# Own slots for the modulation weights in two feed-forward stages of a hybrid backbone kernel

## The chip, the cores and the metric

The kernel is one program on one core of a Trainium2 chip. The metric is device time in microseconds (us) of one execution. TensorE (PE) does the matrix products, VectorE (DVE), ScalarE (ACT) and GpSimd (POOL) the elementwise work, and SyncE (SP) issues all the transfers, in one queue. Each engine runs its instructions in a fixed order: an instruction that waits holds up all that stand behind it on the same engine.

## The reference

Two layers of a diffusion backbone over 256 context tokens and 256 latent tokens of width 1024. Each layer has a feed-forward sub-layer, a token mixer (four branches, one of which is the diagonal state space "S5") and a second feed-forward sub-layer. Every sub-layer is preceded by a modulated norm and followed by a gated norm:

```python
def modulated_norm(x, g, shift, scale):
    return rms_norm(x, g) * (1 + scale) + shift

def swiglu(h, w_in, w_out):
    a, b = jnp.split(h @ w_in, 2, axis=-1)
    return (jax.nn.silu(a) * b) @ w_out

def ffn_sublayer(x, mods, base, g_pre, g_post, w_in, w_out):
    h = modulated_norm(x, g_pre, mods[base], mods[base + 1])
    return x + 0.5 * mods[base + 2] * rms_norm(swiglu(h, w_in, w_out), g_post)
...
    for i in range(DEPTH):
        ...
        mod_l = (act_l @ w_mod[i] + b_mod[i])[:, None, :]
        mod_c = (act_c @ w_mod[i][:, :n_c] + b_mod[i][:n_c])[None, None, :]
```

The shifts, scales and gates (`mods`) are nine vectors of 1024 for the latents; the context has nine in layer 0 and five in layer 1. They come from products of one vector with the columns of `w_mod`. The hidden width of a feed-forward is 2816.

## The kernel before

The program runs the stages one after the other: layer 0's first feed-forward, layer 0's mixer, layer 0's second feed-forward (called **stage B** here, after the pool name in the code), layer 1's first feed-forward (**stage C**), layer 1's mixer, layer 1's second feed-forward. The change touches stages B and C.

A feed-forward stage has a first half over 22 blocks of 128 hidden columns, numbered f (function `ffn`). One block takes two weight chunks (`fin`, 512 KB each, 128x1024), and a product in split precision: each chunk is cut into a high part (`wh`, on ACT, L218) and a low part (`wl`, on DVE, L219), and TensorE makes three products per 128 rows (L225 to L227, tile `pin`): 48 matmuls of 128x512 per block. Then `gate` makes the gated value on ACT and DVE (tiles `t` and `gg`, L484 to L486, L230, L232). The second half (`outproj`, tile `y`) multiplies by the output weights (`foa`, `fob`), and `boundary` adds the residual row (`xr`, loaded from `xd`) and makes the norm for the next stage.

Three loads share this time:

- **The raw ring.** `wchunk` and, before the change, `mod_steps` too take their landing tiles from the same pool (`rp`, tag `raw`, 4 slots). A slot is free again when the work on the tile in it is done; the split tiles `wh` and `wl` have 3 slots each.
- **Modulation products** (`mod_steps`): one step loads a 512 KB piece of `w_mod` and multiplies it with the broadcast activation. In stage B (5 of the 9 vectors, 40 steps) both streams are wanted: the latents' product with its sum is one DVE instruction (tile `jk`, L271), the context's is a product on POOL (L276, in place) and then a sum on ACT (L277), after which the slot is free. In stage C (the other 4, 32 steps) only the latents are wanted: even pieces go to DVE, odd pieces to POOL and ACT. `stepper` hands the steps out by weight: 50 of the stage's 60 units, after two skipped calls.
- **S5 tables** (`s5_tables`, mostly POOL): eight slices, each with four pieces of work ("yields"). The first makes `bb` and `vv` (L1079 to L1090, POOL), the second `wt` (POOL), the third a small TensorE product of `bb` and `vv` (`pn`, L1102) with its copies and `rot`, the fourth turns `wt` on TensorE (L1129), copies it to `row` and stores `row` (1728 KB, `s5tabd`). `row` has one buffer, so the next slice's first write (L1085) waits for that store. `ahead` advances this by one yield per call of `step`, one call for each f.

TensorE's order is the program's own (`manual_schedule`); on the other engines and in SP's queue a scheduler orders the instructions.

Of the kernel before, what the change touches and what calls it, by code (L numbers as in the profile page):

```python
# [9 lines left out]
F32 = mybir.dt.float32  # L10
# [6 lines left out]
P = 128  # L17
D = 1024
KT = 8
# [144 lines left out]
def build(tc, A):  # L164
# [20 lines left out]
    with st, tc.manual_schedule(engines={mybir.EngineType.PE}):  # L185
# [68 lines left out]
            dma(ngt[l], A["ng"][l])  # L254
            dma(bmt[l], A["bmod"][l])

        def mod_steps(l, js, act, raw=None):
            if callable(act):
                act = act()
            for j in js:  # L260
                ss = [1] if l == 1 and j >= 5 else [0, 1]
                for k in range(KT):
                    w = raw() if raw else rp.tile([P, D], F32, tag="raw", name="raw")
                    dma(w, A["wmod"][l, j, k])
                    c = j * KT + k
                    both = l == 0 and j >= JB
                    for s in ss if both else [1]:
                        if 0 not in ss and k % 2:
                            continue
                        jk = sp.tile([P, D], BF16, tag="sq", name="jk", bufs=1)  # L270
                        V.scalar_tensor_tensor(  # L271
                            jk, w, 0.5, act[s], op0=ALU.mult, op1=ALU.mult, accum_out=md[l][:, s, c : c + 1]
                        )
                    if not both and (0 in ss or k % 2):
                        s = ss[0]
                        G.tensor_tensor(w, w, act[s], op=ALU.mult)  # L276
                        S.activation(w, w, AF.Copy, scale=0.5, accum_out=md[l][:, s, c : c + 1])  # L277
                    n = 4 if raw else KT
                    if (k + 1) % n == 0:
                        for s in ss:  # L280
                            m = md[l][:, s, c + 1 - n : c + 1]
                            V.tensor_tensor(m, m, bmt[l][:, c + 1 - n : c + 1], op=ALU.add)
                    yield
# [187 lines left out]

            return run

        def ffn(l, i, h, late, toks, nxt, gp, step, rows, fill, begun=()):
            g = []
            begun = list(begun)
            cs_all = slice(min(toks) * P, NTOK)
# [46 lines left out]
                return gp((n_[0] - 1) // 8).tile([P, 2, 512], F32R, tag="gg", name="wf", bufs=8).rearrange("p a b -> p (a b)")  # L524

            fill()
            return outproj(lhs, NF, A["foa"][l, i], A["fob"][l, i], toks, nxt, lambda: gp(3), place, step)


        xp = pool(st, "xp", 2)  # L530
# [12 lines left out]
        tabd = dp.tile([P, 8, S5_ROW], F32, name="s5tabd")  # L543
        sds = [dp.tile([4, 32, 240], F32, name=f"s5sd{i}") for i in range(8)]

        def ahead(stack, gp, name, slices):

            gp(0)
            gp(1)
            ts = ExitStack()  # L550
            tq = ts.enter_context(tc.tile_pool(name=name, bufs=1, reuse_waits="tile"))
            gen = s5_tables(E, L - 1, slices, tabd, sds, tq, lambda: psy.tile([P, 512], F32, tag="py", name="pn"))

            def close():
                for _ in gen:
                    pass
                ts.close()

            gp.before[2] = close
            return gen  # L560

        def stepper(gens, total, skip=0):

# [32 lines left out]
        with ExitStack() as fs:  # L596
            with ExitStack() as s0:
# [22 lines left out]
                for t in TALL:  # L620
                    xs0[t] = tp.tile([P, D], F32, name=f"x0_{t}")
                raw0 = lambda: tp.tile([P, D], F32, tag="raw0", name="raw0", bufs=RAW0)
                ms0 = mod_steps(0, [0], act, raw0)
                pm = [psy.tile([P, 512], F32, tag="py", name="pm1") for _ in range(2)]

                def rows0(t, load=True):
# [111 lines left out]
        for l in range(L):  # L738
# [8 lines left out]
            with ExitStack() as fs:  # L747
                gp = Gates(fs, f"B{l}")
                if last:
                    n3 = dict(src=xd, out=A["out"], keep=[])  # L750
                    ffn(l, 1, h, late, toks, n3, gp, lambda w: None, lambda: gate_rows(l, 6, 5, 0.5, streams), lambda: None)
                else:
                    n3 = dict(src=xd, out=None, keep=TALL)

                    def fill1():
                        n3.update(coeff=pre_coeff(1, 0, 0, [0, 1]), h=new_h())

                    st1 = stepper([(mod_steps(1, [0, 1, 2, 3, 4], act_load), 40)], 50, 2)
                    tg1 = ahead(fs, gp, "s5p", range(0, 4))

                    def step1(w):
                        st1(w)
                        next(tg1, None)

                    late = ffn(l, 1, h, late, toks, n3, gp, step1, lambda: gate_rows(l, 6, 5, 0.5, streams), fill1)
                    h = n3["h"]
            if not last:
                with ExitStack() as fs:
                    gp = Gates(fs, "C")
                    n4 = dict(src=xd, out=None, keep=TLAT)  # L770

                    def fill2():
                        n4.update(coeff=pre_coeff(1, 3, 2, [0, 1]), h=new_h())

                    st2 = stepper([(mod_steps(1, [5, 6, 7, 8], act_load), 32)], 50, 2)
                    tg2 = ahead(fs, gp, "s5q", range(4, 8))

                    def step2(w):
                        st2(w)
                        next(tg2, None)  # L780

                    late = ffn(1, 0, h, late, TALL, n4, gp, step2, lambda: gate_rows(1, 0, 1, 0.5, [0, 1]), fill2)
                    h = n4["h"]


# [1330 lines left out]
```

## Time and profile before

| | us |
|---|---|
| median of three runs (2684.0 to 2690.7) | 2684.12 |
| the profiled execution | 2686.32 |
| its span, first to last instruction | 2684.5 |
| TensorE busy | 2511.3 (94%) |
| VectorE busy | 1701.1 (63%) |
| ScalarE busy | 1095.2 (41%) |
| GpSimd busy | 792.0 (30%) |

The profiled execution is 2.2 us above the median of the runs. Busy shares are means over stages with different limits; a stage has to be read by itself. TensorE's ends are modelled, so its busy time includes matmuls that ran at the lower of its two clock levels.

### The profile page before, as it was taken

What the parts mean: (1) busy time and instruction counts of PE and PEld (TensorE: products, weight loads), DVE (VectorE), ACT (ScalarE), POOL (GpSimd) and SP (SyncE); (2) the same over time, 40 slices, a digit from 0 to 9 for tenths busy, and PEclk for the clock granted to TensorE, in tenths of its full rate; (3) what the DMA queues carried; (4) which work ended last, traced back from release to release, by engine and by line L of the source; (5) the groups of instructions that cost most, each with busy time, mean ns of one, the idle gap of its engine ahead of it and who ended that gap; (6) DMA issues with size and microseconds to landing.
All of it is one profiled execution on the core that took longest, in us unless ns stands there. A gap on an engine that the chain in (4) does not pass through costs nothing. (4 is left out here: it accounts for less than half of the span.)

```text
span 2684.5 us, 38045 instructions
## 1 busy us (share of the span) xinstructions
PE 2511.3 (94%) x14606; PEld 2105.2 (78%) x14606; DVE 1701.1 (63%) x2488; ACT 1095.2 (41%) x1876; POOL 792.0 (30%) x696
## 2 busy tenths in 40 slices
PE   6978899999999898999888999999999999888998
PEld 3856777888788776888667788887889889788997
DVE  6788885455646798557676646455435567666564
ACT  5435322454543233444343334333334565235443
POOL 4884100100101874007795315554101012000000
PEclk8989999999999999999999999999999999999999
DMA  6345666222232233343554553555532335766564
GB/s 235 107 148 185 210 227 212 83 79 74 78 109 79 77 98 103 94 165 128 183 191 160 175 196 128 182 200 170 196 133 75 95 118 181 263 212 217 158 191 146
DMA packets 137090, 406.87 MB, mean 152 GB/s; under 512 B 27223, under 2 KB 46408, under 8 KB 134092
## 3 DMA queue, kind: packets, MB, share of 16 engines
q1 hardware_dynamic: 136908, 404.44, 45.7%
q8 instruction: 115, 1.88, 0.3%
q14 instruction: 67, 0.55, 0.1%
HBM read 372.31 MB, written 32.06 MB: 151 GB/s over the span
## 5 line engine op out<-in xcount | busy, mean ns | idle before, releaser
L219 DVE TENSOR_TENSOR wl<-raw,wh 128x1024 fp32r<-128x1024 f32 x424 | 572.2, 1350 | 467.7 <-ACT wh L218 461.0
L218 ACT ACTIVATE wh<-raw 128x1024 fp32r<-128x1024 f32 x424 | 447.4, 1056 | 512.8 <-issue 127.4
L227 PE MATMUL pin<-hh,wl 128*128 128x512 f32 (+1 forms) x1468 | 535.0, 364 | 62.1 <-DVE wl L219 62.1
L225 PE MATMUL pin<-hh,wh 128*128 128x512 f32 (+1 forms) x1468 | 534.9, 364 | 12.6 <-DVE hh L353 7.7
L226 PE MATMUL pin<-hl,wh 128*128 128x512 f32 (+1 forms) x1468 | 531.1, 362 | 4.1 <-DVE hl L356 4.0
L227 PEld LDWEIGHTS pin<-hh,wl 128*128 128x128 f32 x1468 | 283.8, 193 | 117.9 <-DVE wl L219 78.2
L246 POOL TENSOR_TENSOR r<-v,mhalf 128x1 f32<-128x1 f32 (+2 forms) x46 | 32.0, 696 | 1046.5 <-DVE v L245 947.9
L225 PEld LDWEIGHTS pin<-hh,wh 128*128 128x128 f32 x1468 | 284.0, 193 | 58.2 <-DVE hh L353 9.2
L276 POOL TENSOR_TENSOR raw<-raw,act 128x1024 f32<-128x1024 f32 x88 | 242.9, 2762 | 266.3 <-DVE jk L271 149.8
L226 PEld LDWEIGHTS pin<-hl,wh 128*128 128x128 f32 x1468 | 284.0, 193 | 46.4 <-DVE hl L356 6.3
L271 DVE SCALAR_TENSOR_TENSOR jk<-raw,act 128x1024 bf16<-128x1024 f32 x152 | 209.0, 1375 | 154.7 <-DMA raw<-wmod 146.6
L1211 PE MATMUL pm<-hh,wh 128*128 128x512 f32 (+1 forms) x704 | 252.2, 358 | 0.0
L1213 PE MATMUL pm<-hh,wl 128*128 128x512 f32 (+1 forms) x704 | 245.5, 349 | 0.8 <-DVE wl L219 0.8
L1212 PE MATMUL pm<-hl,wh 128*128 128x512 f32 (+1 forms) x704 | 245.5, 349 | 0.0
L277 ACT ACTIVATE raw<-raw 128x1024 f32<-128x1024 f32 x88 | 93.2, 1059 | 303.5 <-POOL raw L276 302.2
L400 PE MATMUL y<-wl,gg 128*128 128x512 f32 x448 | 178.1, 398 | 4.3 <-DVE wl L219 4.3
L399 PE MATMUL y<-wh,gg 128*128 128x512 f32 x448 | 177.1, 395 | 0.0
L401 PE MATMUL y<-wh,gg 128*128 128x512 f32 x448 | 177.1, 395 | 0.0
L1211 PEld LDWEIGHTS pm<-hh,wh 128*128 128x128 f32 x704 | 134.4, 191 | 18.4 <-issue 2.7
L1213 PEld LDWEIGHTS pm<-hh,wl 128*128 128x128 f32 x704 | 134.0, 190 | 18.6 <-DVE wl L219 1.0
L1212 PEld LDWEIGHTS pm<-hl,wh 128*128 128x128 f32 x704 | 134.4, 191 | 15.1
L400 PEld LDWEIGHTS y<-wl,gg 128*128 128x128 f32 x448 | 84.1, 188 | 28.3 <-DVE wl L219 8.5
(463 smaller groups left out, 4822.0 us busy)
## 6 DMA issues: line engine op xcount, KB each, us to landing
raw<-fin SPq DMA_DIRECT2D x176, 512.0 KB, 3.6
raw<-wmod SPq DMA_DIRECT2D x136, 512.0 KB, 4.2
raw<-winf SPq DMA_DIRECT2D x122, 512.0 KB, 3.5
raw<-foa SPq DMA_DIRECT2D x64, 512.0 KB, 4.3
raw<-wbr SPq DMA_DIRECT2D x32, 512.0 KB, 3.4
s5tabd<-row SPq DMA_DIRECT2D x8, 1728.0 KB, 7.1
row<-s5tabd SPq DMA_DIRECT2D x8, 1728.0 KB, 7.0
raw<-fob SPq DMA_DIRECT2D x24, 512.0 KB, 4.2
```

What stands on the lines that cost most here:

```text
L218: S.activation(wh, w, AF.Copy)
L219: V.tensor_tensor(wl, w, wh.bitcast(F32), op=ALU.subtract)
L225: T.matmul(out, lhsT=lh, rhs=rh, start=first and i == 0, stop=False)
L226: T.matmul(out, lhsT=lh, rhs=rl, start=False, stop=False)
L227: T.matmul(out, lhsT=ll, rhs=rh, start=False, stop=last and i == n - 1)
L271: V.scalar_tensor_tensor(jk, w, 0.5, act[s], op0=ALU.mult, op1=ALU.mult, accum_out=md[l][:, s, c : c + 1])
L276: G.tensor_tensor(w, w, act[s], op=ALU.mult)
L399: T.matmul(o, lhsT=lh, rhs=rh, start=kt == 0, stop=False)
L400: T.matmul(o, lhsT=lh, rhs=rl, start=False, stop=False)
L1211: T.matmul(o, lhsT=lh, rhs=rh, start=i == 0, stop=False)
L1212: T.matmul(o, lhsT=lh, rhs=rl, start=False, stop=False)
L1213: T.matmul(o, lhsT=ll, rhs=rh, start=False, stop=i == n - 1)
```

## The change

`mod_steps` gets its tiles in stages B and C from a pool of its own with two slots (`mod_ring`, tag `xr`, tile `mraw`). The same two slots later take the first two residual rows, which had a place of their own (`gp(3)`). In layer 1 the latents-only steps do all their products on DVE. The tables are cut into 3 slices in stage B and 5 in stage C instead of 4 and 4, and `go` keeps them to 16 calls: in B some calls advance nothing, in C every fourth call advances two yields.

```diff
-        def mod_steps(l, js, act, raw=None):
+        def mod_steps(l, js, act, raw=None, n=KT):
...
                     for s in ss if both else [1]:
-                        if 0 not in ss and k % 2:
-                            continue
                         jk = sp.tile([P, D], BF16, tag="sq", name="jk", bufs=1)
...
-                    if not both and (0 in ss or k % 2):
+                    if not both and 0 in ss:
                         s = ss[0]
                         G.tensor_tensor(w, w, act[s], op=ALU.mult)
                         S.activation(w, w, AF.Copy, scale=0.5, accum_out=md[l][:, s, c : c + 1])
-                    n = 4 if raw else KT
...
-            return outproj(lhs, NF, A["foa"][l, i], A["fob"][l, i], toks, nxt, lambda: gp(3), place, step)
+            return outproj(lhs, NF, A["foa"][l, i], A["fob"][l, i], toks, nxt, xpool2 or (lambda: gp(3)), place, step)
...
+        def mod_ring(stack, name):
+
+            q = pool(stack, name)
+            return lambda: q, lambda: q.tile([P, D], F32, tag="xr", name="mraw", bufs=2)
...
-            return gen
+            f = [0]
+
+            def go():
+                f[0] += 1
+                for _ in range(len(slices) * f[0] // 4 - len(slices) * (f[0] - 1) // 4):
+                    next(gen, None)
+
+            return go
...
-                    st1 = stepper([(mod_steps(1, [0, 1, 2, 3, 4], act_load), 40)], 50, 2)
-                    tg1 = ahead(fs, gp, "s5p", range(0, 4))
+                    x1, raw1 = mod_ring(fs, "mrB")
+                    st1 = stepper([(mod_steps(1, [0, 1, 2, 3, 4], act_load, raw1), 40)], 50, 2)
+                    tg1 = ahead(fs, gp, "s5p", range(0, 3))
...
-                    st2 = stepper([(mod_steps(1, [5, 6, 7, 8], act_load), 32)], 50, 2)
-                    tg2 = ahead(fs, gp, "s5q", range(4, 8))
+                    x2, raw2 = mod_ring(fs, "mrC")
+                    st2 = stepper([(mod_steps(1, [5, 6, 7, 8], act_load, raw2), 32)], 50, 2)
+                    tg2 = ahead(fs, gp, "s5q", range(3, 8))
```

The scheduler's order moves with it. Below are three places; line numbers of the changed kernel differ from those of before (the product on DVE is L269 there, on POOL L274).

GpSimd in stage B, the beginning of the second table slice; `bb` and `wt` are tiles of the table, `raw` and `mraw` the modulation pieces. Before:

```order
L1086 TENSOR_TENSOR tmp<-s5t,prm 128x576
L276 TENSOR_TENSOR raw<-raw,act 128x1024
L205 TENSOR_TENSOR wt<-s5t,bb 128x512
L208 TENSOR_TENSOR wt<-s5t,bb 128x512
L276 TENSOR_TENSOR raw<-raw,act 128x1024
L1085 TENSOR_TENSOR row<-s5t,prm 128x576
```

The same place in the changed kernel:

```order
L1097 TENSOR_TENSOR tmp<-s5t,prm 128x576
L274 TENSOR_TENSOR mraw<-mraw,act 128x1024 x5
L205 TENSOR_TENSOR wt<-s5t,bb 128x512
L208 TENSOR_TENSOR wt<-s5t,bb 128x512
L274 TENSOR_TENSOR mraw<-mraw,act 128x1024
L1096 TENSOR_TENSOR row<-s5t,prm 128x576
```

Where one product stood between two table operations there are now five: the steps are no longer tied to the weight chunks and stand earlier. All 40 stand before the 40th `wl` of the 44 on DVE; before, 29 of them did, and the rest stood between the last chunks and in the second half. On GpSimd 21 of the 40 stand in runs with no large table operation between them (the last run has 11), the other 19 among the three slices' table operations.

SP's queue in stage C, around the store of the stage's first table slice. Before:

```order
L176 DMA raw<-wmod 128x1024
L176 DMA s5tabd<-row 128x3456
L176 DMA raw<-fin 128x1024 x2
L176 DMA raw<-wmod 128x1024
L176 DMA prm<-s5bc 128x256
L176 DMA raw<-fin 128x1024 x2
L176 DMA raw<-wmod 128x1024
L176 DMA s5t<-s5d_109 128x276
L176 DMA raw<-fin 128x1024 x2
```

In the changed kernel:

```order
L176 DMA mraw<-wmod 128x1024 x2
L176 DMA raw<-fin 128x1024
L176 DMA s5tabd<-row 128x3456
L176 DMA mraw<-wmod 128x1024 x2
L176 DMA raw<-fin 128x1024
L176 DMA mraw<-wmod 128x1024
L176 DMA raw<-fin 128x1024
L176 DMA mraw<-wmod 128x1024
L176 DMA prm<-s5bc 128x256
L176 DMA mraw<-wmod 128x1024
L176 DMA raw<-fin 128x1024
```

One or two pieces of `w_mod` now stand between two weight chunks, where there was one piece per two chunks; on DVE the first 8 of the stage's 32 products stand ahead of the first block's gated value and all 32 ahead of the eighth block's; before, 5 and 10 did, and 7 pieces were still loaded behind the last weight chunk of the first half.

VectorE at the start of stage C, from the last residual row's norm to the first `wl` that stands behind it (`h` to `hl` are the tiles that TensorE waits for). Before:

```order
L324 TENSOR_SCALAR xn<-xr,r 128x512
L350 TENSOR_SCALAR h_13601<-pt,pa,md_96 128x128 x4
L353 CAST hh<-h_13594 128x4x128
L356 TENSOR_TENSOR hl<-h_13594,hh 128x4x128
L356 TENSOR_TENSOR hl<-h_13601,hh 128x4x128
L219 TENSOR_TENSOR wl<-raw,wh 128x1024
L485 SCALAR_TENSOR_TENSOR t<-t,pin 128x512
```

In the changed kernel:

```order
L321 TENSOR_SCALAR xn<-xr,r 128x512
L269 SCALAR_TENSOR_TENSOR jk,md_96<-mraw,act 128x1024
L347 TENSOR_SCALAR h_13529<-pt,pa,md_96 128x128 x4
L269 SCALAR_TENSOR_TENSOR jk,md_96<-mraw,act 128x1024
L350 CAST hh<-h_13522 128x4x128
L353 TENSOR_TENSOR hl<-h_13529,hh 128x4x128
L353 TENSOR_TENSOR hl<-h_13522,hh 128x4x128
L269 SCALAR_TENSOR_TENSOR jk,md_96<-mraw,act 128x1024 x3
L219 TENSOR_TENSOR wl<-raw,wh 128x1024
L482 SCALAR_TENSOR_TENSOR t<-t,pin 128x512
```

Two products now stand between `xn` and the two `hl`, and three more ahead of the `wl`.

## Rows read from the trace of the kernel before

**Rows 1.** The page: busy us, share of the span, instructions.

```profile
PE 2511.3 (94%) x14606; PEld 2105.2 (78%) x14606; DVE 1701.1 (63%) x2488; ACT 1095.2 (41%) x1876; POOL 792.0 (30%) x696
```

**Rows 2.** Busy us (count) of each engine by stretch, granted clock, DMA share, GB/s.

```profile
1221.79:1440.00 218.21, 194.97 (x997) 157.58 (x996) 159.35 (x155) 86.73 (x152) 185.58 (x132) 0.96 0.48 164
...
1221.79:1517.37 295.58, 265.10 (x1286) 213.47 (x1284) 211.13 (x212) 117.00 (x198) 210.89 (x142) 0.96 0.49 169
1517.37:1642.79 125.42, 124.95 (x546) 100.37 (x544) 63.13 (x83) 48.12 (x79) 26.32 (x14) 1.00 0.51 168
1642.79:1906.77 263.98, 254.74 (x1307) 211.17 (x1306) 141.84 (x168) 96.98 (x163) 142.64 (x123) 0.99 0.54 182
```

**Rows 3.** Waits in stage B's first half: us in total, times, longest.

```profile
ACT raw L277 <- POOL raw L276: 120.9, 32, 9.0
...
DVE jk L271 <- DMA raw<-wmod: 56.8, 26, 5.0
...
PE pin L227 <- DVE wl L219: 23.2, 17, 3.9
```

**Rows 4.** Groups in stage B's first half, DVE and POOL: count, busy us, mean ns.

```profile
L219 DVE TENSOR_TENSOR wl<-raw,wh 128x1024 fp32r<-128x1024 f32 x41 | 79.7, 1945 | 18.8 <-ACT wh L218 18.8
L271 DVE SCALAR_TENSOR_TENSOR jk<-raw,act 128x1024 bf16<-128x1024 f32 x33 | 51.6, 1564 | 54.9 <-DMA raw<-wmod 54.6 <-DMA act<-actd 0.3
...
L276 POOL TENSOR_TENSOR raw<-raw,act 128x1024 f32<-128x1024 f32 x33 | 93.7, 2838 | 75.3 <-DVE jk L271 72.1 <-DMA s5t<-s5d 2.0 <-ACT raw L277 1.2
```

**Rows 5.** Timeline in stage B, one product's way round: start us, us.

```profile
1470.64 2.40 POOL L276 TENSOR_TENSOR raw<-raw,act 128x1024 f32<-128x1024 f32 x1 [1.82 <-DVE jk L271]
...
1470.99 3.14 DVE L219 TENSOR_TENSOR wl<-raw,wh 128x1024 fp32r<-128x1024 f32 x1 [0.48 <-ACT wh L218]
...
1474.16 0.33 SPq L176 DMA_DIRECT2D raw<-wmod  x1
...
1477.61 1.23 DVE L271 SCALAR_TENSOR_TENSOR jk<-raw,act 128x1024 bf16<-128x1024 f32 x1 [2.88 <-DMA raw<-wmod]
...
1482.84 0.42 SPq L176 DMA_DIRECT2D raw<-wmod  x1
...
1483.51 1.23 DVE L219 TENSOR_TENSOR wl<-raw,wh 128x1024 fp32r<-128x1024 f32 x1 [0.48 <-ACT wh L218]
```

**Rows 6.** Groups in stage C's first half, DVE.

```profile
L219 DVE TENSOR_TENSOR wl<-raw,wh 128x1024 fp32r<-128x1024 f32 x42 | 61.6, 1466 | 51.6 <-ACT wh L218 51.6
L232 DVE TENSOR_TENSOR gg<-t,gg 128x512 fp32r<-128x512 f32 x21 | 20.1, 955 | 0.8 <-ACT gg L230 0.8
L271 DVE SCALAR_TENSOR_TENSOR jk<-raw,act 128x1024 bf16<-128x1024 f32 x14 | 19.1, 1362 | 34.9 <-DMA raw<-wmod 34.9
L486 DVE SCALAR_TENSOR_TENSOR t<-t,pin 128x512 f32<-128x512 f32 x21 | 14.4, 684 | 9.1 <-PE pin L227 8.0
```

**Rows 7.** Busy in a stretch of full pace in stage C (columns as rows 2).

```profile
1940.00:1960.00 20.00, 20.00 (x88) 16.10 (x87) 4.90 (x4) 4.24 (x4) 0.00 (x0) 1.00 0.28 93
```

**Rows 8.** Waits in stage C's first half.

```profile
PE pin L227 <- DVE wl L219: 4.1, 4, 1.3
```

**Rows 9.** Timeline in stage C, from one table slice to the next.

```profile
1743.55 1.03 PE L1129 MATMUL pn<-ident,wt 128*128 128x128 f32 x8
...
1767.16 1.43 POOL L1090 TENSOR_TENSOR row<-row,tmp 128x576 f32<-128x576 f32 x1
...
1789.22 1.03 PE L1129 MATMUL pn<-ident,wt 128*128 128x128 f32 x8
...
1818.42 1.42 POOL L1090 TENSOR_TENSOR row<-row,tmp 128x576 f32<-128x576 f32 x1
```

**Rows 10.** Timeline in stage C: a modulation piece's issue and its product.

```profile
1689.02 0.33 SPq L176 DMA_DIRECT2D raw<-wmod  x1
...
1693.11 1.22 DVE L271 SCALAR_TENSOR_TENSOR jk<-raw,act 128x1024 bf16<-128x1024 f32 x1 [3.06 <-DMA raw<-wmod]
```

More of the change, by code (lines that the diff above doesn't have):

```diff
@@ L472, in unit, with ffn @@
             return run
-        def ffn(l, i, h, late, toks, nxt, gp, step, rows, fill, begun=()):
+        def ffn(l, i, h, late, toks, nxt, gp, step, rows, fill, begun=(), xpool2=None):
             g = []
@@ L622, in build @@
                 raw0 = lambda: tp.tile([P, D], F32, tag="raw0", name="raw0", bufs=RAW0)
-                ms0 = mod_steps(0, [0], act, raw0)
+                ms0 = mod_steps(0, [0], act, raw0, 4)
                 pm = [psy.tile([P, 512], F32, tag="py", name="pm1") for _ in range(2)]
@@ L756, in fill1 @@
                         n3.update(coeff=pre_coeff(1, 0, 0, [0, 1]), h=new_h())
-                    st1 = stepper([(mod_steps(1, [0, 1, 2, 3, 4], act_load), 40)], 50, 2)
-                    tg1 = ahead(fs, gp, "s5p", range(0, 4))
+                    x1, raw1 = mod_ring(fs, "mrB")
+                    st1 = stepper([(mod_steps(1, [0, 1, 2, 3, 4], act_load, raw1), 40)], 50, 2)
+                    tg1 = ahead(fs, gp, "s5p", range(0, 3))
                     def step1(w):
                         st1(w)
-                        next(tg1, None)
-                    late = ffn(l, 1, h, late, toks, n3, gp, step1, lambda: gate_rows(l, 6, 5, 0.5, streams), fill1)
+                        tg1()
+                    late = ffn(l, 1, h, late, toks, n3, gp, step1, lambda: gate_rows(l, 6, 5, 0.5, streams), fill1, xpool2=x1)
                     h = n3["h"]
@@ L773, in fill2 @@
                         n4.update(coeff=pre_coeff(1, 3, 2, [0, 1]), h=new_h())
-                    st2 = stepper([(mod_steps(1, [5, 6, 7, 8], act_load), 32)], 50, 2)
-                    tg2 = ahead(fs, gp, "s5q", range(4, 8))
+                    x2, raw2 = mod_ring(fs, "mrC")
+                    st2 = stepper([(mod_steps(1, [5, 6, 7, 8], act_load, raw2), 32)], 50, 2)
+                    tg2 = ahead(fs, gp, "s5q", range(3, 8))
                     def step2(w):
                         st2(w)
-                        next(tg2, None)
-                    late = ffn(1, 0, h, late, TALL, n4, gp, step2, lambda: gate_rows(1, 0, 1, 0.5, [0, 1]), fill2)
+                        tg2()
+                    late = ffn(1, 0, h, late, TALL, n4, gp, step2, lambda: gate_rows(1, 0, 1, 0.5, [0, 1]), fill2, xpool2=x2)
                     h = n4["h"]
```

## The prediction

> **What bounds the kernel now.** The page comes first. TensorE is busy 94% of the span [rows 1], so nothing that leaves TensorE's work alone can bring more than the remaining idle time and the time at the lower clock. Next the busy time by stretch, to see where that idle time lies. Stages B and C do the same work with different weights, 22 blocks of 48 matmuls each, so C is the measure for B: B's first half takes 295.6 us, C's takes 264.0 us [rows 2]. TensorE is idle for 30.5 us of B's stretch (295.58 - 265.10) and for 9.2 us of C's. In B's second half it is idle for half a microsecond, so there is nothing to win there. Full pace is seen in a stretch of C: 88 matmuls in 20 us [rows 7], or 10.9 us for a block and 5.45 us for one weight chunk.
>
> The waits tell why B is slow. TensorE waits 23.2 us for `wl`. Behind that, ACT stands 120.9 us in front of the product on POOL, and DVE 56.8 us in front of a modulation piece that has not landed [rows 3]. The weight chunk's split stands behind these on both engines. POOL is full while the table slices last: busy 185.6 of 218.2 us to 1440, which is 85% [rows 2].
>
> **The change in stage B.** What is removed: the modulation pieces leave the ring of four, so weight chunks no longer wait for them; one of four table slices goes. What is moved: the 40 products stand earlier, all ahead of the 40th `wl`, so TensorE's 40th chunk waits for all of them at the latest. What is added: two slots that a product holds all the way round. I take the path of the products first, then TensorE behind it.
>
> One way round with POOL free is 1474.16 to 1482.84, from one issue to the next issue, 8.7 us, with 1.23 us on DVE and 2.4 us on POOL [rows 5]. With the stage's mean durations, 1.56 and 2.84 us [rows 4], it is 9.5 us, and two slots give a product every 4.75 us. The 21 products without table operations between them take 21 x 4.75 = 100 us. The other 19 share POOL with three slices. A slice costs (210.9 - 93.7) / 4 = 29 us of POOL [rows 2, 4], so that part has 19 x 2.84 + 3 x 29 = 141 us of POOL work. If POOL never idled there, the sum would be 241 us; the last product's POOL and ACT part (4 us) is not waited for, the `wl` behind it adds 2 us, and the last five chunks take 5 x 5.45 = 27 us: 266 us, or 30 us less than the 295.6 us of before. That is nearly the pace of C. If POOL idles as much as now (85%), the 141 us become 166 us and the stage takes 291 us: 5 us less. The old kernel had one product between two table operations and the queue ran dry whenever DVE was late; now five stand in a row, which keeps it fuller, but two slots alone still empty it. I take 92%: 153 us, a stage of 278 us, **17 us won**, with 5 and 30 as ends.
>
> The residual rows now wait until both slots are done with products. In the first half's last four blocks there are none left, and the second half lasts 125.4 us [rows 2]: these loads cost nothing. Without that cover a load of about 4 us [rows 10] would stand ahead of the boundary.
>
> **The change in stage C.** Removed: 16 POOL products and 16 ACT sums. They caused TensorE's 4.1 us of waiting for `wl` [rows 8]: **4 us won**, nothing at worst. Three costs stand against it.
>
> First, the products themselves. Between the first and the eighth gated value DVE has 24 of them, 3.4 a block. A block costs DVE 2 x 1.47 (`wl`), 2 x 0.68 (`t`), 0.96 (`gg`) and 3.4 x 1.44 (product and reading its sum, the latter 0.08 us), which is 10.2 of 10.9 us [rows 6, 7]. So it fits with 0.7 us a block, 5 us in seven blocks. A `wl` can be made two chunks before its use, 10.9 us, less its own ACT and DVE time some 8 us: lateness up to 13 us in all is hidden. What eats this is DVE waiting for pieces. The two slots turn in 4.1 us from issue to product [rows 10] plus 1.4 us, so one every 2.8 us, against 3.2 us wanted (10.9 / 3.4): on the mean no wait, at best. Now DVE waits 34.9 us for 14 products, 2.5 us each [rows 6]; so 24 x 2.5 - 13 = 47 us at worst. The demand for slots is close to the supply, as at the lower end, but the queue is in order and the transfers collide with a table store: I take 0.7 us each, 17 - 13 = **4 us lost**.
>
> Second, the tables. Five slices in 16 calls: the small product (L1102) of slices two to four stands two blocks (21.8 us) behind the turning of `wt` of the slice before; it stood three (32.7 us). Between the two events `row` is copied, stored, and rewritten by POOL. From the start of the turning to the end of POOL's last write of `vv` it was 25.0 us (1743.55 to 1768.59) and 30.6 us (1789.22 to 1819.84) [rows 9]. So far this was hidden behind three blocks; with two it is 3.2 and 8.8 us too long. A product of 2.4 us on POOL, which lay in the way, is gone: 0.8 to 6.4 us a slice, 2 to 19 us for three, or nothing where TensorE is late for the first reason anyway. Near the lower end, as ACT's copies too stood behind a sum: **3 us lost**.
>
> Third, the start. Two products of 1.36 us [rows 6] stand ahead of the last two `hl`: 0 to 2.7 us; I take **1 us**.
>
> The fifth slice's own TensorE work leaves B and comes to C; that is even.
>
> **Sum.** -17 in B, -4 + 4 + 3 + 1 = +4 in C: 13 us less. The profiled execution took 2686.3 us (span 2684.5 and 1.8 around it), 2.2 above the median of the runs; on the median it is 2684.1 - 13 = **2671 us**.
>
> **A rule beside a row.** A `wl` that began 0.35 us after a product on POOL took 3.14 us and ended 1.09 us behind it, where one with POOL free took 1.23 us [rows 5]. The Trainium skill's page "SBUF — State Buffer", section "Who interferes with whom", says that a DVE instruction with two inputs in SBUF and a GpSimd one that reads SBUF exclude each other, the later one blocked for the whole of the earlier. The row agrees. By this rule each microsecond of POOL work that leaves a stage gives DVE up to as much back; by that the 2 us that a `wl` loses here would shrink with the slice that leaves, and the sum would be the first rival's below. My sum keeps the mean durations as they are and gives nothing back.
>
> **Rivals.**
>
> *Stage B runs at C's pace.* With 29 us of POOL work less, DVE in B is blocked less. The mean `wl` there is 1.95 us against 1.23 us free [rows 4, 5]: 0.7 us for each of two a block. If that goes, POOL's products are blocked less too, and the 30 us end is reached, with C losing 2: 2684 - 30 + 2 = 2656 us. Against it: the products that remain stand closer together. Chance 0.15. It is the exclusion of the Trainium skill's page "SBUF — State Buffer" that would give this.
>
> *The ring eats the gain.* Two slots held through DVE, POOL and ACT empty POOL's queue as much as now, 85%: 5 us won in B, 4 lost in C: 2683 us, no change. For it: four slots, if shared, did no better. Chance 0.2.
>
> *Stage C's products wait.* Each waits for its piece on DVE nearly as long as now, say 2.2 us: 24 x 2.2 - 13 = 40 us lost, with -17 in B and the other terms 0: 2684 + 23 - 4 = 2703 us. It turns the sign from a wait of 1.4 us on (24 x 1.4 - 13 = 21 = 17 + 4). For it: slots wanted every 3.2 us and given every 2.8 us leave little, and weight chunks and table stores share the queue. Against it: DVE's own work between two products gives a piece most of the time to land. Chance 0.2.
>
> **How the numbers follow.** The forecast has 0.45. A measurement of this kernel can tell about 0.3%, 8 us, from no change: faster is below 2676. Forecast and first rival are faster, less a part of the forecast's lower edge, but with the better part of the second rival's upper one: 0.58. The second rival and that edge: 0.22. Slower 0.20. The range holds 2656 and, of the slow rival, the nearer half: 2654 to 2698 us; the forecast's own range is 2660 to 2680.
>
> **What would show it.** In B: the first half at some 278 us instead of 295.6, TensorE's wait for `wl` below 12 us, the wait of ACT for POOL still the largest. If B's first half is above 290, the ring held it. In C: `jk` waiting for `mraw` for some 20 us; more than 35 us, with TensorE waiting for `wl` in the first eight blocks, is the slow rival. TensorE waiting for POOL at L1102's place (L1113 in the new numbering) three times would be the tables. A first half of C above 275 us makes the forecast wrong, and so does a second half of B that waits for `xr`.

## The result and the profile after

The changed kernel takes 2705.8 us (median of 4 runs, 2702.4 to 2708.2) against 2686.5 us before (4 runs): ratio 1.0068, 95% interval 1.0050 to 1.0086. It is slower, and outside the forecast's range. The profiled execution took 2703.5 us, with a span of 2701.7.

The page first. VectorE has 30 us more to do than in [rows 1], POOL 42 us and ScalarE 15 us less; TensorE's busy time is up by 2.4 us for the same 14606 matmuls.

```profile
PE 2513.7 (93%) x14606; PEld 2109.5 (78%) x14606; DVE 1731.0 (64%) x2520; ACT 1080.6 (40%) x1844; POOL 749.7 (28%) x680
```

The busy time by stretch, columns as in [rows 2]: stage B up to the 1434th us and to the end of its first half, its second half, and stage C's first half.

```profile
1213.00:1434.20 221.20, 193.53 (x962) 156.67 (x961) 180.95 (x176) 93.73 (x161) 176.92 (x115) 0.96 0.51 173
1213.00:1510.10 297.10, 264.38 (x1266) 213.87 (x1265) 231.97 (x234) 124.93 (x208) 198.73 (x123) 0.97 0.54 184
1510.10:1634.20 124.10, 124.10 (x545) 100.88 (x544) 45.45 (x61) 39.54 (x63) 3.41 (x7) 1.00 0.36 120
1634.20:1920.00 285.80, 262.71 (x1347) 217.12 (x1346) 174.38 (x210) 86.44 (x145) 141.58 (x136) 0.96 0.57 189
```

B's first half takes 297.1 us from its first product on. In the kernel before, counted in the same way from 1219.0 us, it took 298.4 (the forecast began 2.8 us later and had 295.6). So nothing was won in B, where 17 us were forecast. POOL is no fuller than before: 176.9 of 221.2 us is 80%, against 85% in [rows 2]. C's first half takes 285.8 us instead of 264.0: 21.8 us lost, where 4 were forecast. TensorE's idle time in C is 23.1 us (it was 9.2), and its work of the same kind takes longer, at a granted clock of 0.96. The rest of the program, whose code is unchanged, differs by some microseconds from one execution to the next (the stretch between C's first half and the last stage took 579 to 589 us in the kernels below), so stages are compared and not only spans.

The waits in B's first half, as in [rows 3]:

```profile
ACT mraw L275 <- POOL mraw L274: 117.5, 36, 5.8
...
DVE jk L269 <- DMA mraw<-wmod: 25.8, 16, 4.7
...
PE pin L227 <- DVE wl L219: 22.8, 12, 5.3
```

VectorE waits half as long for pieces (56.8 us in [rows 3]), but TensorE waits for `wl` as long as before (23.2). The groups answer to [rows 4]: 40 products now lie in this half, and a `wl` is no shorter.

```profile
L219 DVE TENSOR_TENSOR wl<-raw,wh 128x1024 fp32r<-128x1024 f32 x43 | 86.0, 2002 | 26.3 <-ACT wh L218 23.2 <-DMA mraw<-wmod 3.0
L269 DVE SCALAR_TENSOR_TENSOR jk<-mraw,act 128x1024 bf16<-128x1024 f32 x40 | 69.8, 1745 | 26.6 <-DMA mraw<-wmod 25.8 <-DMA act<-actd 0.8
L274 POOL TENSOR_TENSOR mraw<-mraw,act 128x1024 f32<-128x1024 f32 x40 | 110.4, 2760 | 59.5 <-DVE jk L269 45.1 <-ACT mraw L275 7.3 <-ACT wh L218 4.6
```

The waits in C's first half ([rows 8] before). `wl` costs TensorE 0.9 us and no longer 4.1. In its place stand 14.6 us for POOL at the small product (L1113), and behind them POOL's own waits until the row of the slice before has been stored.

```profile
POOL row L1096 <- DMA s5tabd<-row: 41.9, 4, 18.0
...
DVE jk L269 <- DMA mraw<-wmod: 21.1, 12, 5.9
PE pn L1113 <- POOL row L1098: 9.3, 2, 5.2
...
PE pn L1113 <- POOL row L1101: 5.3, 2, 3.3
...
PE pin L227 <- DVE wl L219: 0.9, 1, 0.9
```

One of these waits, followed back through the engines' timelines (start, duration, engine, what it waited for):

```profile
1693.99 0.58 ACT L1141 ACTIVATE row<-pn 128x512 f32<-128x512 f32 x1
1695.20 2.10 DVE L269 SCALAR_TENSOR_TENSOR jk<-mraw,act 128x1024 bf16<-128x1024 f32 x1 [2.79 <-DMA mraw<-wmod]
...
1702.16 0.68 DVE L483 SCALAR_TENSOR_TENSOR t<-t,pin 128x512 f32<-128x512 f32 x1
1702.87 0.63 ACT L230 ACTIVATE gg<-t 128x512 fp32r<-128x512 f32 x1 [8.30 <-DVE t L483]
1703.41 0.58 ACT L1141 ACTIVATE row<-pn 128x512 f32<-128x512 f32 x1
1704.42 0.38 SPq L176 DMA_DIRECT2D s5tabd<-row  x1
...
1714.19 1.18 POOL L1096 TENSOR_TENSOR row<-s5t,prm 128x576 f32<-128x576 f32 x1 [17.97 <-DMA s5tabd<-row]
...
1718.71 2.31 POOL L1098 TENSOR_TENSOR row<-row,tmp 128x576 f32<-128x576 f32 x1
...
1721.07 0.65 PE L1113 MATMUL pn<-row,bb 64*32 64x128 f32 x8 [5.23 <-POOL row L1098]
```

The two ScalarE copies of one slice's `row` (L1141) stand 9.4 us apart. Between them in ScalarE's queue is a `gg` that waits 8.3 us for `t`, and `t` stands in VectorE's queue behind products, two of which waited for their pieces (2.79 and 0.74 us). The store goes when the second copy is done, POOL may rewrite `row` only when the store has landed, and TensorE's next small product is 5.2 us late. [Rows 9] of before show both ends of the same chain; there the two copies of a slice began 0.5 and 1.2 us apart.

Two slices' small products were late, by 8.5 and 6.2 us over their two parts. The second one went another way:

```profile
1741.42 1.07 ACT L1141 ACTIVATE row<-pn 128x512 f32<-128x512 f32 x2
...
1747.95 2.33 SPq L176 DMA_DIRECT2D mraw<-wmod  x2
1750.38 0.37 SPq L176 DMA_DIRECT2D s5tabd<-row  x1
...
1767.80 0.65 PE L1113 MATMUL pn<-row,bb 64*32 64x128 f32 x8 [4.09 <-POOL row L1098]
```

Here the two copies follow each other and are done at 1742.5, but the store is issued 7.9 us later: it stands in SyncE's queue behind two pieces that wait for a slot, which a product on VectorE has to free. So two queues hold the row back, ScalarE's behind `t` and SyncE's behind the pieces, both times behind modulation products that run early.

### The profile page after: what moved, and what is told of

It is laid out like the page before. It is cut to its first block, busy times and chain, and to the rows that moved or that the text cites. A ratio compares the mean times of both kernels' runs of the same rounds, so it can differ in the third digit from the quotient of the medians.

```text
span 2701.7 us, 38022 instructions
## 1 busy us (share of the span) xinstructions
PE 2513.7 (93%) x14606; PEld 2109.5 (78%) x14606; DVE 1731.0 (64%) x2520; ACT 1080.6 (40%) x1844; POOL 749.7 (28%) x680
## 5 line engine op out<-in xcount | busy, mean ns | idle before, releaser
L225 PEld LDWEIGHTS pin<-hh,wh 128*128 128x128 f32 x1468 | 285.8, 195 | 59.7 <-DVE hh L350 9.8
L269 DVE SCALAR_TENSOR_TENSOR jk<-raw,act 128x1024 bf16<-128x1024 f32 x96 | 127.9, 1332 | 42.5 <-DMA raw<-wmod 34.5
L269 DVE SCALAR_TENSOR_TENSOR jk<-mraw,act 128x1024 bf16<-128x1024 f32 x72 | 119.2, 1655 | 47.8 <-DMA mraw<-wmod 46.8
L274 POOL TENSOR_TENSOR mraw<-mraw,act 128x1024 f32<-128x1024 f32 x40 | 110.4, 2760 | 59.5 <-DVE jk L269 45.1
L274 POOL TENSOR_TENSOR raw<-raw,act 128x1024 f32<-128x1024 f32 x32 | 88.1, 2757 | 63.4 <-DVE jk L269 59.6
```

What stands on the lines that cost most here:

```text
L225: T.matmul(out, lhsT=lh, rhs=rh, start=first and i == 0, stop=False)
L269: V.scalar_tensor_tensor(jk, w, 0.5, act[s], op0=ALU.mult, op1=ALU.mult, accum_out=md[l][:, s, c : c + 1])
```

## The experiments

Each kernel was timed in turns with the kernel before. "B" and "C" are the first halves of the two stages, from the first product to the first `y`, in the profiled execution (before: 298.4 and 264.0 us; changed: 297.1 and 285.8). The same code of a stage gives times some 3 us apart: B is as in the changed kernel in tables_spread, paced_c and late_sum (296.0 to 298.5), C is one code in paced_c, paced_bc and dense_half (257.8 to 260.9). Smaller differences are not read.

| run | whole, us | ratio to before (95%) | B, us | C, us |
|---|---|---|---|---|
| tables_even | 2702.7 | 1.0058 (1.0041 to 1.0075) | 308.9 | 272.3 |
| tables_only | 2686.7 | 1.0000 (0.9990 to 1.0010) | 294.6 | 267.0 |
| tables_spread | 2695.0 | 1.0033 (1.0020 to 1.0047) | 296.0 | 279.0 |
| late_sum | 2702.2 | 1.0054 (1.0034 to 1.0073) | 298.5 | 284.3 |
| dve_only | 2687.9 | 1.0000 (0.9989 to 1.0010) | 298.7 | 263.4 |
| paced_c | 2677.8 | 0.9965 (0.9953 to 0.9976) | 296.1 | 257.8 |
| spread_paced_bc | 2645.3 | 0.9845 (0.9832 to 0.9859) | 263.8 | 258.9 |
| even_paced_bc | 2652.1 | 0.9877 (0.9862 to 0.9892) | 272.5 | 256.2 |
| before_paced | 2678.6 | 0.9960 (0.9948 to 0.9973) | 290.5 | 256.6 |
| paced_bc | 2644.8 | 0.9832 (0.9818 to 0.9847) | 263.6 | 260.2 |
| paced_dense | 2677.6 | 0.9961 (0.9946 to 0.9976) | 279.4 | 278.4 |
| paced_late | 2643.7 | 0.9826 (0.9809 to 0.9844) | 263.5 | 258.2 |
| between_t | 2662.4 | 0.9902 (0.9885 to 0.9918) | 269.9 | 264.1 |
| dense_half | 2651.0 | 0.9866 (0.9849 to 0.9883) | 268.0 | 260.9 |

### The tables alone, and the change without them

tables_even undoes the split of the tables in the changed kernel; tables_only makes that split alone in the kernel before.

```
-tg1 = ahead(fs, gp, "s5p", range(0, 3))      # tables_even; tables_only the other way round,
+tg1 = ahead(fs, gp, "s5p", range(0, 4))      # with go() from the change
-tg2 = ahead(fs, gp, "s5q", range(3, 8))
+tg2 = ahead(fs, gp, "s5q", range(4, 8))
```

> The changed kernel, with the tables back at four and four slices, one part a block in both stages; the two slots and the products on VectorE stay. Theory (tables): the small product of a slice again stands three blocks behind the turning of wt, so stage C's first half falls from 285.7 to 264 to 270 us, TensorE waits for POOL there under 2 us in all, and the clock of the stage is back at 0.99. Stage B has a slice more: its first half becomes 297 to 312. Whole: 2684 to 2700 us. Rival (products): the 24 products that wait for their pieces on VectorE are the cause; then C stays at 280 or more and the whole above 2700.

> The kernel before, with one part of the change alone: three slices in stage B and five in C, with the 16 calls that share out their parts. Ring of four shared, products on POOL as before. Theory (tables): C's first half goes from 264.0 to 279 to 290 us, with TensorE waiting for POOL at the small product of slices two to four for 10 us or more; B's first half, a slice of 29 us of POOL work less, gets 5 to 15 us shorter than 295.6. Whole: 2680 to 2705 us. Rival (products): C within 5 us of 264, whole 2670 to 2680.

Neither theory holds by itself. The split alone costs C 3.0 us (267.0 - 264.0), no more than two executions can differ by, but with this wait at the small product:

```profile
PE pn L1109 <- POOL row L1097: 4.7, 2, 4.0
```

Slots and products alone cost C 8.3 us (272.3 - 264.0), with none of these waits above 0.3 us: 5.1 us are idle time of TensorE (14.3 against 9.2), 3.2 its own work at a lower clock (258.0 against 254.7). Together they cost 21.8: the other 10.5 us come only from both. In B, the slots alone cost 10.5 us (308.9 against 298.4), a slice less wins 3.8 with the old ring and 11.8 with the new.

### The same work with the next small product a block later

```
+if len(slices) == 5:                 # calls 3, 6, 9, ...: small product, turning, next row
+    n = {1: 1, 2: 1, 0: 3}[f[0] % 3] if f[0] < 3 else {0: 3, 1: 1, 2: 0}[f[0] % 3]
```

> The changed kernel, with five slices in stage C as it has them, but the calls regrouped: the turning of wt stands right behind the small product of the same slice, so that the next small product stands three blocks behind it (blocks 3, 6, 9, 12, 15). The work is the same to the last instruction. Theory (tables): TensorE's waits for POOL in C (14.65 us) go to under 3, C's first half to 264 to 272 us, the whole to 2684 to 2692. If the whole chain, not its place, is too long, one or two waits of 2 to 5 us are left and C stands at 272 to 280. Rival (products): C stays at 280 or more.

Half of the tables' part comes back, 6.8 us in C (279.0 us, where the theory had 264 to 272), and the wait for POOL at the small product is gone. TensorE's wait then moves to the weights, which the tables theory didn't expect:

```profile
PE pin L227 <- DVE wl L219: 10.8, 4, 5.6
```

So VectorE is late in C for more than the tables.

### ScalarE's sums a step later: inconclusive

```
-S.activation(w, w, AF.Copy, scale=0.5, accum_out=...)   # in the step itself
+todo.append((w, s, c, None))                            # summed in the next step
```

> The changed kernel, but in stage B ScalarE sums each POOL product one step later, when the next piece's product has been issued, so that ScalarE does not stand before a product that POOL is still working off (117.5 us in 36 waits in stage B). Theory (ScalarE's queue): these waits hold the weight chunks' copies back, and wl with them; B's first half falls from 297 to 270 to 282 us, the whole to 2680 to 2692. Rival (slots): the two slots are held one step longer, the pieces come later, and VectorE waits for them: B stays at 292 or more, or gets longer. Rival (POOL): it is POOL's own work and VectorE's exclusion with it: B within 5 us of 297 and wl still near 2 us each. Stage C is as in the changed kernel, 286 us.

B did not move, but nor did the wait:

```profile
ACT mraw L268 <- POOL mraw L287: 117.3, 36, 6.7
```

The order of the queues is made when the program is built, for every engine but TensorE, and it put the sums back where they had stood: ScalarE's queue in B reads as in the changed kernel, instruction by instruction. The run says nothing on that queue, beyond a second time for the changed kernel. paced_late, the same edit in a faster version, has the same flaw.

> The changed kernel with the products behind the second t in both stages, the table parts regrouped in C, and ScalarE's sum of a POOL product one step later in B. With the order right, ScalarE still stands 103.5 us before POOL's products in B, and TensorE waits 9.6 us in that half. Theory (ScalarE's queue counts once VectorE's is in order): B 257 to 261 us, whole 2638 to 2643. Rival (hidden, as in the changed kernel): B within 2 us of 263.8, whole within 4 us of 2645.

Its time is that of paced_bc.

### The products behind the second t

VectorE's queue is the next suspect. In the changed kernel the products depend on nothing but their own two slots, and they stand far ahead of where the code has them: in C 8 of the 32 ahead of the first block's `gg` and the other 24 ahead of the eighth's, in B all 40 in some 18 blocks. This is VectorE's queue in the third block of C in the changed kernel:

```
L269 SCALAR_TENSOR_TENSOR jk,md_96<-mraw,act 128x1024
L219 TENSOR_TENSOR wl<-raw,wh 128x1024
L482 SCALAR_TENSOR_TENSOR t<-t,pin 128x512
L269 SCALAR_TENSOR_TENSOR jk,md_96<-mraw,act 128x1024 x2
L483 SCALAR_TENSOR_TENSOR t<-t,pin 128x512
L219 TENSOR_TENSOR wl<-raw,wh 128x1024
L269 SCALAR_TENSOR_TENSOR jk,md_96<-mraw,act 128x1024
L232 TENSOR_TENSOR gg<-t,gg 128x512
```

In the next kernel, paced_c, it reads `wl`, `t`, `t`, `jk`, `wl`, `gg`. The edit holds a step's product on VectorE behind the second `t` of its block, and what needs that product (the slot, POOL's product, ScalarE's sum) moves with it; in paced_c for stage C only. dve_only is the third part of the change alone, in the kernel before.

```
+mark["g"] = V.scalar_tensor_tensor(t, ..., ps[1], ...)   # second t, in gate()
-    st2(w)
+    with after(mark["g"]):
+        st2(w)
```

> The changed kernel, with one thing added in stage C: each modulation piece's step is placed behind the second t of its block, so that VectorE's queue reads wl t t J wl gg as in a block of before, where in the changed kernel 24 of the 32 products (J) stand in the first seven blocks, up to three of them ahead of a t. Tables three and five, two slots and the products on VectorE stay. Theory (VectorE's queue): the early products hold t back, with t the ScalarE copy of the table row behind it, with the copy the row's store, and with the store POOL's rewrite and TensorE's small product; then C's first half falls from 285.7 to 264 to 271 us (267.0 with five slices and the old ring) and the whole to 2684 to 2692, B unchanged at 297. Rival (slots): two slots and the chain over two blocks are too short in any order: C stays at 276 or more.

> The kernel before, with one part of the change alone: in stage C all 32 products of the latents on VectorE (16 stood on POOL with a ScalarE sum). Shared ring of four, tables four and four. Theory (VectorE's queue): the shared ring itself spreads the products, one or two a block over the whole stage, so they hold no t back for long: C's first half 261 to 269 us, the whole within 6 us of before. Rival (VectorE's time): 16 products of 1.4 us more on VectorE are what costs; then C is at 270 to 276, as with two slots and four slices (272.3).

paced_c turns the loss in C into a gain of 6.2 us against before: 257.8 us, less than the 264 to 271 expected. Slots, slices and the small product two blocks behind are as they were. TensorE waits at no small product, and VectorE never for a piece. SyncE's queue moved too: each store is now issued within 0.5 us of its row's second copy, and 25 products lie in the first half, 7 in the second. So the run shows that the place and pace of the products are the cause in C; it does not part VectorE's queue from SyncE's.

```profile
1636.40:1894.20 257.80, 253.94 (x1346) 211.47 (x1345) 171.83 (x194) 86.64 (x144) 145.29 (x136) 1.00 0.57 193
```

```profile
POOL row L1097 <- DMA s5tabd<-row: 16.7, 4, 5.5
```

Of the 28.0 us between the two stages C, 19.2 are idle time of TensorE (23.1 against 3.9) and 8.8 its own work at a lower clock (262.7 against 253.9 for the same matmuls). dve_only shows that more products on VectorE cost the first half nothing while the shared ring spreads them: 263.4 us (C's second half is 128.5 us there, 124.3 in all the other runs). And it shows that waiting is not yet a loss. VectorE stands longer for pieces there, and ScalarE longer for `t`, than in the changed kernel (21.1 and 32.7 us):

```profile
DVE jk L269 <- DMA raw<-wmod: 78.3, 25, 8.8
ACT gg L230 <- DVE t L484: 49.5, 12, 8.2
```

With four slices and one or two products a block, none of this reaches TensorE's small product.

### The same in stage B

spread_paced_bc holds the products in both stages and has the tables regrouped as in tables_spread; paced_bc has them as in the changed kernel; even_paced_bc has four and four slices; before_paced holds the products in the kernel before.

```
-    st1(w)
+    with after(mark["g"]):
+        st1(w)
```

> The changed kernel with the product steps placed behind the second t of their block in both stages, and the table parts in C regrouped so that a small product stands three blocks behind the turning of the slice before. Theory (VectorE's queue, both stages): C's first half 262 to 268 us; B, where the early products stand ahead of t and wl too, falls from 297 to 280 to 290 us; the whole to 2668 to 2684. Rival (POOL in B): POOL's table parts and products and their exclusion with VectorE set B's pace, not the place of the products: B 293 to 300, the whole 2680 to 2690. Against both: the last six products of B now stand in its second half, which gets longer than 126 us if the residual rows then wait for the slots.

> As the run with the products behind the second t in both stages, but with the tables at four and four slices, one part a block. Theory (VectorE's queue): C's first half 262 to 267 us; B with a slice more than the 3 and 5 split, by the 4 us that a slice cost there with the old ring (298.4 against 294.6): 284 to 294. Whole 2670 to 2688. If the whole stands within 3 us of the 3 and 5 version, the split is worth nothing in either direction. Rival (POOL in B): B 300 or more, as with two slots and four slices before (308.9).

> The kernel before, none of the change, but with the product steps of both stages placed behind the second t of their block in VectorE's queue (in the old code too most products of stage B stand between or ahead of the two t). Theory (the queue alone): B falls from 298 to 262 to 275 us and the whole to 2645 to 2662, as in the changed kernel with that order; the change itself is then worth next to nothing either way. Rival (queue and slots): with the four slots shared, a weight chunk stands behind a product's piece, POOL product and sum in the ring, so B stays at 285 or more and the whole at 2672 or more; then the change's own slots are worth the difference to 2645.

> The changed kernel with the products behind the second t in both stages and nothing else: tables three and five with the small product two blocks behind the turning. Theory: with the queue in order the two blocks are enough, as stage C alone showed (257.8 us, no wait for POOL at the small product): C 256 to 261, B 263 to 267, whole 2642 to 2649. Rival: the regrouped calls gave part of the gain: C 264 or more, whole 2652 or more.

B came out shorter than expected in spread_paced_bc (263.8 against 280 to 290) and even_paced_bc (272.5 against 284 to 294); before_paced came out as its rival had it, and paced_bc within its ranges. paced_bc is the fastest but for what the intervals can't tell apart: 0.9832, 43.6 us under the 2688.4 of before in the same rounds. The table parts needed no regrouping. The busy time in its B (both halves) and C:

```profile
1214.90:1478.50 263.60, 254.07 (x1266) 210.70 (x1265) 216.47 (x208) 114.90 (x190) 175.62 (x114) 0.99 0.55 182
1478.50:1602.60 124.10, 124.10 (x545) 101.06 (x545) 69.08 (x88) 49.59 (x81) 27.58 (x16) 1.00 0.51 175
1602.60:1862.80 260.20, 256.38 (x1347) 214.19 (x1346) 167.91 (x194) 86.53 (x145) 145.78 (x136) 0.99 0.57 191
```

The waits in B's first half of paced_bc are 5.8 us where the changed kernel has 22.8, and 3.4 where it has 25.8. ScalarE's wait of 103.6 us is nearly what it was (117.5), and TensorE is idle for only 9.5 us beside it:

```profile
ACT mraw L275 <- POOL mraw L274: 103.6, 31, 8.0
...
PE pin L227 <- DVE wl L219: 5.8, 4, 2.2
...
DVE jk L269 <- DMA mraw<-wmod: 3.4, 3, 2.3
```

Nine of the 40 products now lie in the second half, which takes 124.1 us with no idle time of TensorE; the residual rows that share the slots cost nothing there. With the same edit the old kernel takes 2678.6 us, 33.7 more. Its queue on VectorE is not quite the same: in most blocks of B a `wl` stands between the two `t`. Its chunks share the ring with the pieces and are not there when ScalarE wants them, a wait that paced_bc doesn't have:

```profile
ACT wh L218 <- DMA raw<-fin: 55.0, 24, 4.5
```

So with the products held the slots are worth 18.0 us in B (290.5 to 272.5, four slices each) and 4.1 in its second half (128.2 to 124.1). The split of the tables is worth 8.9 in B and costs some 2 to 5 in C (257.8 to 260.9, against 256.2).

### Place or number

paced_bc changes two things, the place of a product and how many there are in a block. paced_dense keeps the place but lets the products come nearly as fast as in the changed kernel (in C all 32 in eleven blocks, not thirteen as its expectation has it); between_t keeps the number and puts the product between the two `t`; dense_half is dense in B but makes both products of every second piece on VectorE, so that POOL has 20 instead of 40.

```
-st1 = stepper([(mod_steps(...), 40)], 50, 2)    # paced_dense, dense_half
+st1 = stepper([(mod_steps(...), 40)], 40, 0)    # st2 in paced_dense: 20, 0
...
-both = l == 0 and j >= JB                       # dense_half
+both = l == 0 and j >= JB or l == 1 and j < 5 and k % 2
...
+mark["g"] = V.scalar_tensor_tensor(t, ..., ps[0], ...)   # between_t: first t,
+step(2)                                                  # the step,
+with after(mark["j"]):                                   # the second t behind the product
```

> The changed kernel with the products placed behind t, but as dense as the changed kernel has them: in stage C all 32 in the first thirteen blocks, mostly two a block and a few between the two t, in B all 40 in the first half. Theory (order): what counts is that t does not stand behind a product that waits for its piece; C stays at 264 us or less and B at 262 to 272; whole 2642 to 2660. Rival (density): VectorE's and the queue's share of time in the dense blocks counts: C 270 or more and B 280 or more, whole 2670 or more.

> The changed kernel with as many products a block as in the run that reached 2645 us (1.5 in B, 1.3 in C), but standing between the two t of a block instead of behind the second; tables three and five. Theory (place): a product that stands ahead of a t holds it back wherever it waits; B 275 to 292 us, C 266 to 280, whole 2662 or more. Theory (number a block): when no more products are asked for than POOL and the two slots can turn in a block, the piece has landed when its turn comes and the place is of no account; B 262 to 269, C 256 to 264, whole 2640 to 2655.

> The changed kernel with the products behind the second t, in C 1.3 a block, in B two pieces a block from the first block on as in the dense run (279.4 us there), but for every second piece of B both products on VectorE, so that POOL and ScalarE have 20 products there instead of 40. Theory (POOL): two products of 2.8 us and its share of three slices, 5.4 us, are 11 us of POOL in a block of 10.9, so POOL can't turn the slots in time; with one a block it has 8.2 us: B 262 to 270 us, whole 2640 to 2655. Rival (VectorE): its queue is what is full, and one product of 1.3 us more a block makes it longer: B 278 or more, whole 2662 or more.

Both count. paced_dense came out close to its rival, dense_half as its theory had it, and between_t between its two theories, with B at 269.9 and C at 264.1 us. From the changed kernel's two halves of B together (421.2 us), the place alone wins 17.7 (paced_dense, 403.5), the number alone 20.9 (between_t, 400.3, with the product between the two `t` and not where the changed kernel has it), both 33.5 (387.7). In C the number alone wins 21.7 (264.1); the place could not be had alone there, since at two to three products a block some still stand between the two `t`. With the number kept and the place wrong, the pieces are waited for again, in B of between_t:

```profile
DVE jk L269 <- DMA mraw<-wmod: 29.2, 12, 6.8
```

What the number costs in B is told by paced_dense and dense_half, B's first half of each, and `wl` in it:

```profile
1214.20:1493.60 279.40, 261.76 (x1266) 214.97 (x1266) 243.55 (x234) 124.56 (x208) 202.61 (x123) 0.96 0.57 192
...
L219 DVE TENSOR_TENSOR wl<-raw,wh 128x1024 fp32r<-128x1024 f32 x43 | 86.0, 2000 | 20.6 <-ACT wh L218 20.6
```

```profile
1215.40:1483.40 268.00, 255.58 (x1267) 212.42 (x1266) 242.58 (x274) 103.02 (x169) 161.48 (x103) 0.97 0.61 204
...
L219 DVE TENSOR_TENSOR wl<-raw,wh 128x1024 fp32r<-128x1024 f32 x43 | 61.1, 1421 | 6.4 <-ACT wh L218 6.4
```

VectorE is busy as long in both (243.6 and 242.6 us), yet the second is 11.4 us shorter: a full VectorE is not the price. POOL has 41 us less and ScalarE 22, as 20 sums went with the products; `wl` is 0.58 us shorter on the mean, and waits 14 us less for `wh`. The run doesn't part POOL from ScalarE. Nor does the stage follow the length of `wl`: it is 1.90 us in paced_bc's B, which is 4.4 us shorter still, and 1.56 us in before_paced's, which takes 290.5.

```profile
L219 DVE TENSOR_TENSOR wl<-raw,wh 128x1024 fp32r<-128x1024 f32 x43 | 81.7, 1900 | 25.4 <-ACT wh L218 25.2
```

## Why the prediction was wrong

**What is moved, in stage B.** This is the step that failed. The prediction had seen that "the 40 products stand earlier", and took from it only that the 40th `wl` comes behind the last of them. It then priced POOL's share ("I take 92%") and the slots' way round. But a product that stands early in VectorE's queue is also a wait ahead of some `t` and `wl`. The 17 us became 1.3. Two terms of its sum were short. In the last run of products, with no table operation between them, they came every 5.5 us, not every 4.75, and the last one left POOL 266.7 us after the stage's start, where the sum has 253 and its lower end 266:

```profile
1422.20 3.26 POOL L274 TENSOR_TENSOR mraw<-mraw,act 128x1024 f32<-128x1024 f32 x1 [1.23 <-DVE jk L269]
...
1477.00 2.72 POOL L274 TENSOR_TENSOR mraw<-mraw,act 128x1024 f32<-128x1024 f32 x1 [2.36 <-DVE jk L269]
```

And what stood behind it took 30.4 us, not 25. But this path need not have set the stage's length. In paced_dense the last product leaves POOL later still, 272.7 us after the start, and the stage is 17.7 us shorter, 279.4: there a product has its piece when its turn comes (`jk` waits 3.7 us for pieces, not 25.8).

```profile
1484.52 2.40 POOL L274 TENSOR_TENSOR mraw<-mraw,act 128x1024 f32<-128x1024 f32 x1 [1.83 <-DVE jk L269]
```

With the products behind `t` and 1.5 a block the same slots give 263.6 us, 34.8 under before, past the upper end of 30. The term was not wrong in what slots and slices can bring, but in the order that it took for free. That order failed the sum in stage C too, in the next terms.

**The rule beside the row.** The long `wl` of [rows 5] stays long as long as POOL is busy with products: 2.00 us at 40 of them, 1.42 us at 20. This agrees with the exclusion that the Trainium skill's page "SBUF — State Buffer", section "Who interferes with whom", states. The number of products is not all, though: with 31 of them it was 1.90 us in paced_bc and 1.56 in before_paced. The prediction kept the mean as it was, and so it came: the slice that left B did not shorten `wl` (2.00 us).

**Stage C, removed.** TensorE's wait for `wl` fell from 4.1 to 0.9 us: 3.2 of the 4 us, much as forecast.

**Stage C, the products.** The sign to look for was some 20 us of `jk` waiting for pieces; it was 21.1. But its price was sought at `wl`, against a slack of 13 us. Most of it was paid at the table row: its copy stands behind a `gg` that waits for `t`, its store behind pieces that wait for a slot. The prediction had ScalarE's copies in the tables' term, as something that gets earlier ("ACT's copies too stood behind a sum").

**Stage C, the tables.** Forecast 3 us, 2 to 19. The term is right alone (3.0 in tables_only, if a difference as small as that can be read) and four times too small in company: 13.5 us (285.8 - 272.3), within its range. Costs that share queues were added as if they did not.

**The start.** 3.00 us of waiting for `hl` instead of 1.10: 1.9, forecast 1, within its bounds.

**The rivals.** "The ring eats the gain" named B's outcome, but two slots are enough when the order is right. "Stage C's products wait" gave 2703 us, near what was measured, for another reason: not 40 us at `wl`, but 21.8 in C, most of it at the tables, and nothing won in B. That 24 products stand in seven blocks was known and priced by the mean pace of two slots; that the place and the number could be chosen was not asked.

What stays open: how much of B's loss ScalarE's waits before POOL carry, since the sums could not be moved in its queue; with 103.6 us of them paced_bc has TensorE idle in B for 9.5 us. In C VectorE's queue was not parted from SyncE's, the place was not tried without the number, and two combinations were not run: the slots without the products on VectorE, and those products with five slices and the old ring.

## What to carry to other kernels

Work that is given its own buffers loses the order that the shared buffers had imposed: look where it stands in each in-order queue now, and what stands behind it, before pricing the work itself. If it runs ahead, tie it to a place behind the work that the critical engine needs, at a rate that the engines on its way can turn; here a tie of that kind in both stages was worth 61 us, where the change without it cost 19. And test parts of a change in pairs: two of the three here left the time as it was when made alone (1.0000 both).

## What the runs showed of the hardware

Waits of TensorE can cost more than their own length. In the changed kernel's C the granted clock was 0.99 to 1.00 from 1700 to 1720 us, with TensorE busy 5.8 of the last ten; in the ten after that it was 0.50, the lower of its two levels (1.2 of 2.4 GHz):

```profile
1700.00:1710.00 10.00, 10.00 (x45) 8.26 (x44) 8.04 (x12) 2.55 (x4) 0.00 (x0) 1.00 0.88 302
1710.00:1720.00 10.00, 5.84 (x26) 4.50 (x24) 4.59 (x5) 3.46 (x6) 5.81 (x7) 0.99 0.75 283
1720.00:1730.00 10.00, 5.67 (x41) 3.98 (x42) 10.00 (x8) 1.49 (x3) 9.61 (x6) 0.50 0.70 199
```

Over the stage this made 8.8 us, against 19.2 us of idle time: nearly half as much again, which the sum of waits in the prediction did not hold. It is no fixed rate: in C of the kernel before, 9.2 us of idle time went with a granted clock of 0.99 [rows 2].
